# Second feed-forward product before the inner norms: the second tile's own block product is moved from ahead of the last rows to behind the first tile's

## The chip, the core and the metric

The kernel runs on one core of one Trainium2 chip. The metric is the device time of one execution in microseconds (us). Before the change it is 1187.21 us, the median of 3 runs (1186.62 to 1187.24). "Tile" means 128 of the 256 tokens: the first tile is tokens 0 to 127, the second 128 to 255. "Matmul" is one TensorE instruction; in the profile TensorE is PE (its weight loads PEld), VectorE DVE, ScalarE ACT, GpSimd POOL, and SyncE SP.

## The reference, cut to what matters

Two layers of three blocks each. The change concerns the feed-forward block, which is run four times, and the layer norm behind it:

```python
def _swiglu(x, w1, w3, w2):
    return (jax.nn.silu(x @ w1) * (x @ w3)) @ w2

for l in range(DEPTH):                                   # DEPTH = 2
    h = _swiglu(x, ffn_w1[l, 0], ffn_w3[l, 0], ffn_w2[l, 0])
    x = _layernorm(ALPHA * x + 0.5 * h, ln_g[l, 0], ln_b[l, 0])
    h = _mixer(x, ...)                                   # gated token mixers
    x = _layernorm(ALPHA * x + h, ln_g[l, 1], ln_b[l, 1])
    h = _swiglu(x, ffn_w1[l, 1], ffn_w3[l, 1], ffn_w2[l, 1])
    x = _layernorm(ALPHA * x + 0.5 * h, ln_g[l, 2], ln_b[l, 2])
```

x is 256 x 1024, the inner width 2816 (22 blocks of 128). The layer norm is over the 1024 features of a token, so it needs a token's whole row before it can scale any of it.

## The kernel before, in words

**Number format.** Each product is made of three: both operands are split into a high part (float32r) and the rest, and high x high, low x high and high x low are added in PSUM. ACT writes a weight block's high part (`whi`), DVE its low part (`wlo`); both live in two pools of 8 buffers. Weights come by DMA from SP's queue into 4 `raw` buffers.

**The second product of a feed-forward block** is `gemm_seven` (L380). Its output is 2 tiles x 2 halves of 512 columns, collected in four PSUM banks `q[half][tile]`. The first 8 of the 22 inner blocks are done as 2 x 2 blocks with seven products in place of eight (`product`, L372: 12 matmuls of 128x512 each, of which the text calls one a *block product*). One of the sums goes through a side bank `bx`: its value is added on DVE into the token rows `y = xtok` by `ln.fold` (L626), and the last of them, `product(bx, a22, pieces(r1), ...)` with the `fold(1, 0, ...)` behind it, concerns the second tile's first half alone. The other 14 inner blocks are plain rows (`rows`, L405): one call is one weight piece for one tile, 6 matmuls. For the second half of the columns there are 7 such pieces, `rest(1)`; they are all made first (`held`), then the first tile runs over all 7 (42 matmuls), then the second tile (42 matmuls).

**The norm.** `done` calls `Norm.part` (L640): a half of the product is added to `y` on DVE (L647, SCALAR_TENSOR_TENSOR) and its statistics are taken (L651, BN_STATS). With a tile's second half comes `Norm.finish` (L655): BN_AGGR, an inverse square root in small DVE steps (L255 to L261), and the scaled rows (L667). The first tile's first 512 features are turned by four PE transposes (L714), its other half and the second tile's two halves by transposing DMAs (L220, `moved`). Then `affine` (L745) writes the next stage's input `x`: ACT applies gain and bias (L762) and writes the high part (L247), DVE the low part (L249). `self.xlo[0, 0]` is the DVE instruction that writes the low part of the first tile's first 512 features; `part` puts the addition of a second half behind it.

**What comes next.** Behind three of the four feed-forward blocks stands another stage, and its first product (`gemm_b2`, L467, rows by `rows_b` L314, matmuls L283) reads that `x` as the stationary operand: 48 matmuls for the first tile, the first 24 of them over its first 512 features, then 48 for the second tile. The order of instructions on PE is written out by hand; on the other engines it is made by a scheduler that follows priorities, dependences and the `behind` marks. `beat` advances a clock, counted in matmuls, by which the norm's later steps are put between the matmuls.

Of the kernel before, what the change touches and what calls it, by code (L numbers as in the profile page):

```python
# [17 lines left out]
ALU = mybir.AluOpType  # L18
# [5 lines left out]
NT = T // P  # L24
# [30 lines left out]
def trunk(ctx, tc, x, xT, w13a, w13b, w2, wb, wqk, wu, wg, wgr, wbr, wbrr, wo, gateb, gatebr, sgug, sgub, sguwT, sgubias, lam, diffg,  # L55
          lng, lnb, lngT, lnbT, cosT, sinT, out):
    nc = tc.nc
    V, A, G, PE = nc.vector, nc.scalar, nc.gpsimd, nc.tensor
# [15 lines left out]
    def name(s):  # L74
        serial[0] += 1
        return f"{s}_{serial[0]}"

    def bank():
        return psum.tile([P, 512], F32, tag="main", name=name("bank"))

    def side_bank():
        return psum.tile([P, 512], F32, tag="side", name=name("sbank"))
# [41 lines left out]
    def beat(w):  # L124

        clock[0] += w
        for task in list(tasks):
            if task[0] <= clock[0]:
                turn(task)
# [20 lines left out]
    def inline(eng, ins):  # L150
        if line[2]:
            line[eng is V] = ins
        return ins

    def behind(ins):

        return tc.issue_after(ins) if ins is not None else nullcontext()
# [87 lines left out]
    def split(hi, lo, src, eng=V, after=(None, None)):  # L245
        with behind(after[0]):
            a = A.activation(hi, src, AF.Copy).ins  # L247
        with behind(after[1]):
            return a, eng.tensor_tensor(out=lo, in0=src, in1=hi.bitcast(F32), op=ALU.subtract).ins  # L249
# [97 lines left out]
    def halved(v):  # L347
        return v if isinstance(v, list) else [v[:, o : o + HC] for o in range(0, CH, HC)]
# [13 lines left out]
    def pieces(raw):  # L362
        out = []
        for v in halved(raw):
            hi = hi_pool.tile([P, HC], F32R, tag="hi", name=name("whi"))
            lo = lo_pool.tile([P, HC], F32R, tag="lo", name=name("wlo"))
            for eng, ins in zip((A, V), split(hi, lo, v, after=line[:2])):
                inline(eng, ins)
            out.append((hi, lo))
        return out  # L370

    def product(ps, x, w, start, stop):  # L372
        for k in range(4):
            hi, lo = (v[:, k % 2 * 512 : k % 2 * 512 + 512] for v in w[k // 2])
            for n, (y, o) in enumerate(((hi, 0), (lo, 0), (hi, 1))):
                PE.matmul(ps, x[o](k), y, start=start and k == n == 0, stop=stop and k == 3 and n == 2,  # L376
                          skip_group_check=True)
            beat(0.25)

    def gemm_seven(src, xh, xl, sums, ln, done):  # L380

        q = [[bank(), bank()], [side_bank(), bank()]]  # L390
        bx, bz = side_bank(), q[1][0]
        (w11, w21), (w12, w22) = ([s[:, o : o + CH] for o in (0, CH)] for s in src)

        def rest(c):
            for k in range(8, FT, 4):
                nk = min(4, FT - k)
                if c:
                    for j, piece in enumerate(stream(src[c][:, k * 512 : (k + nk) * 512], nk * 512)):
                        yield k + 2 * j, piece
                    continue  # L400
                raw = fetch(src[c][:, k * 512 : (k + nk) * 512], nk * 512)
                for o in range(0, nk * 512, HC):
                    yield k + o // 512, pieces([raw[:, o : o + HC]])[0]

        def rows(t, c, k0, piece, o=0, n=512):  # L405
            for j in range(2):
                k = k0 + j
                hi, lo = (w[:, j * 512 + o : j * 512 + o + n] for w in piece)
                for m, (y, x) in enumerate(((hi, xh), (lo, xh), (hi, xl))):
                    PE.matmul(q[c][t][:, :n] if o == 0 else more[:, :n], x(k, t), y,  # L410
                              start=k == 8 and m == 0 and (c, t) != (1, 0) and not o, stop=k == FT - 1 and m == 2, skip_group_check=True)
            beat(n / 1024)

        def block(t, k0):
            return tuple(lambda k, f=f: f(k0 + k, t) for f in (xh, xl))

        a11, a12, a22 = block(0, 0), block(0, 4), block(1, 4)
        first = rest(0)

        def between():  # L420
            k, piece = next(first)
            for t in range(NT):
                rows(t, 0, k, piece)

        r1 = fetch(w11)
        p1 = pieces(r1)
        r2 = fetch(w12, raw=homes(hi_pool, "hi"))
        product(bx, a11, p1, True, False)
        ln.fold(0, 0, bx, ALU.add, True)
        between()  # L430
        p2 = pieces(fetch(w21))
        plus(r1, r2)
        product(q[0][0], a12, p2, False, False)
        gather(r2, w22)
        r3 = fetch(w22, raw=homes(lo_pool, "lo"))
        between()
        product(bz, sums[0], pieces(r1), True, False)
        ln.fold(1, 1, bz, ALU.add, True)
        between()
        product(bx, sums[1], pieces(plus(r1, r3)), False, False)  # L440
        ln.fold(0, 1, bx, ALU.subtract, True)
        gather(r1, w21)
        between()
        product(bz, sums[3], pieces(r3), False, False)
        between()
        product(bx, sums[2], pieces(r2), False, False)
        ln.fold(1, 1, bx, ALU.subtract, False)
        between()
        between()
        product(bx, a22, pieces(r1), False, True)  # L450
        ln.fold(1, 0, bx, ALU.add, True)
        for t in range(NT):
            done(t, q[0][t], 0, 512)
        held = list(rest(1))
        line[:] = None, None, False
        cuts = ((0, 512),), (((0, 256), (256, 256)) if ln.last else ((0, 512),))
        for t in range(NT):
            for o, n in cuts[t]:
                more = bank() if o else None
                if o:  # L460
                    for m, x in enumerate(ln.kept()):
                        PE.matmul(more[:, :n], ln.unit, x, start=m == 0, stop=False, skip_group_check=True)
                for k, piece in held:
                    rows(t, 1, k, piece, o, n)
                done(t, (more if o else q[1][t])[:, :n], 512 + o, n)

    def gemm_b2(srcs, xh, xl, done, norm=None, second=(0, 1), each=None):  # L467
# [126 lines left out]
    class Norm:  # L594
# [5 lines left out]

        def __init__(self, l, i, scale, eps, after, last=False):
            self.scale, self.eps, self.last, self.done, self.front = scale, eps, last, set(), i
            self.ends, self.xhi, self.xlo, self.rows = [None] * NT, {}, {}, {}
            self.gT, self.bT = (v[:, l, i] for v in (ln_g, ln_b))
            self.y = x_tok
            self.group = 256 if last else 512
            self.st = [sm("st", D // self.group * 6, bufs=2) for _ in range(NT)]
            self.g, self.b = bc_load(lng[l, i], after), bc_load(lnb[l, i], after)
            if last:
                beside(self.halved(), 9)  # L610
                self.minus = s512("minus")
                A.activation(self.minus[:, :P], ident, AF.Copy, scale=-1.0)
                self.eps_t = self.minus[:, 2 * P : 2 * P + 1]
                V.memset(self.eps_t, eps)
                with behind(silu[0]):
                    A.activation(sm("first", 1), mask[:, :1], AF.Sqrt)
            else:
                self.via = []
                self.x = [xs.tile([P, 4, 512], F32R, tag="x", name=name("x")) for _ in range(2)]
# [20 lines left out]
        def part(self, t, c, ps, folded=False):  # L640
            s = slice(c, c + ps.shape[1])
            if self.last and (t, s.stop) == (NT - 1, D):
                V.bn_stats(out=self.st[t][:, c // self.group * 6 : c // self.group * 6 + 6], in_=ps)  # L643
                self.end = ps
                return
            with behind(self.xlo.get((0, 0)) if c else None):
                V.scalar_tensor_tensor(out=self.y[t][:, s], in0=self.y[t][:, s], scalar=1.0 if folded else self.scale,  # L647
                                       in1=ps, op0=ALU.mult, op1=ALU.add)
            for o in range(s.start, s.stop, self.group):
                g = o // self.group * 6  # L650
                V.bn_stats(out=self.st[t][:, g : g + 6], in_=self.y[t][:, o : o + self.group])  # L651
            if self.last and t == NT - 1 and s.stop < D:
                V.tensor_tensor(out=self.y[t][:, s], in0=self.y[t][:, s], in1=self.g[:, s], op=ALU.mult)

# [703 lines left out]
```

## Time and profile before

| | |
|---|---|
| time, median of 3 runs | 1187.21 us (1186.62 to 1187.24) |
| the profiled execution's own time | 1186.85 us |
| its span in the trace | 1185.1 us |
| granted TensorE clock, mean | 1.00 |
| where the three inner `gemm_seven` end and the next stage begins | about 180.4, 591.9 and 766.8 us |
| the last `gemm_seven` (not changed) ends the kernel | from about 1120 us on |

The profile has a page and views of the trace. A line of a timeline gives start, duration, engine, source line, operation, output<-input, and the number of instructions merged into the line; in brackets stands the idle time before it and what ended it. A line of the chain gives start, duration, and what was on the path that ended last; the duration there is net, so that matmuls following each other without a gap show their spacing. Matmul durations in a timeline overlap, since matmuls are pipelined. The time of the execution lies 1.75 us above its span.

### The profile page before, as it was taken

How to read it: one execution, taken by the hardware profiler on the slowest of the kernel's cores; microseconds unless marked ns; L12 is line 12 of the kernel's file. 1: busy time of each engine (PE TensorE's matmuls, PEld its weight loads, DVE VectorE, ACT ScalarE, POOL GpSimd, SP SyncE). 2: the span in 40 equal slices, each digit the busy share in tenths (PEclk: the TensorE clock that was granted, in tenths of full speed). 3: DMA queues.
4: the chain of work that ended last, by engine and by line, in shares of the span. 5: the costliest groups of instructions: out<-in, count | busy, mean ns of one | idle time of the engine just before them, and what ended most of it. 6: DMA issues, size and time to landing. Idle time of an engine off the chain costs nothing.

```text
span 1185.1 us, 16676 instructions
## 1 busy us (share of the span) xinstructions
PE 1180.5 (100%) x5777; PEld 995.0 (84%) x5777; DVE 1013.1 (85%) x1562; ACT 828.1 (70%) x1419; POOL 287.5 (24%) x350
## 2 busy tenths in 40 slices
PE   9999999999999999999999999999999999999998
PEld 8888888888888888888888888888888888888887
DVE  6989989788688989889899889888965989988895
ACT  6688658559955677876667876576788556679761
POOL 1011201247420220051020161003564112102600
PEclk9999999999999999999999999999999999999999
DMA  9869976767865658699668689586666755786881
GB/s 355 265 198 262 287 273 208 266 193 238 246 205 173 227 188 273 187 275 267 239 220 265 190 278 280 198 290 232 212 204 208 250 181 174 247 254 208 273 260 36
DMA packets 129621, 275.10 MB, mean 232 GB/s; under 512 B 89041, under 2 KB 90369, under 8 KB 105473
## 3 DMA queue, kind: packets, MB, share of 16 engines
q1 hardware_dynamic: 121968, 248.67, 63.5%
q0 software_dynamic: 6992, 24.71, 8.7%
q8 instruction: 45, 0.74, 0.2%
q10 hardware_dynamic: 576, 0.66, 0.2%
q14 instruction: 40, 0.32, 0.1%
HBM read 248.05 MB, written 1.05 MB: 210 GB/s over the span
## 4 chain that ended last, share of the span: by engine, by line
PE 99%; DVE 0%; DVEq 0%; issue 0%
PE bank L283 46%; PE bank L295 15%; PE sbank L376 12%; PE bank L410 10%; PE bank L302 8%; PE sbank L410 3%; PE bank L530 2%; PE sbank L1017 1%; PE bank L376 1%; PE sbank L1073 1%; PE sbank L1191 1%; PE sbank L542 0%; PE sbank L1071 0%; PE sbank L714 0%; DVE xtok L701 0%; DVE st L643 0%
## 5 line engine op out<-in xcount | busy, mean ns | idle before, releaser
L197 DVE TENSOR_TENSOR wlo<-raw,whi 128x1024 fp32r<-128x1024 f32 (+1 forms) x346 | 379.4, 1123 | 51.8 <-ACT whi L195 38.0
L195 ACT ACTIVATE whi<-raw 128x1024 fp32r<-128x1024 f32 (+1 forms) x350 | 323.4, 952 | 135.1 <-PE bank L283 43.0
L283 PE MATMUL bank<-whi,x 128*128 128x512 f32 x1224 | 386.4, 390 | 0.0
L283 PEld LDWEIGHTS bank<-whi,x 128*128 128x128 f32 x1224 | 229.8, 188 | 47.8
L283 PE MATMUL bank<-wlo,x 128*128 128x512 f32 x612 | 238.2, 389 | 0.0
L249 DVE TENSOR_TENSOR wlo<-raw,whi 128x1024 fp32r<-128x1024 f32 (+1 forms) x123 | 142.9, 1185 | 20.3 <-ACT whi L247 11.4
L247 ACT ACTIVATE whi<-raw 128x1024 fp32r<-128x1024 f32 (+1 forms) x123 | 121.1, 1003 | 51.2 <-DVE raw L359 23.9
L295 PE MATMUL bank<-x,whi 128*128 128x512 f32 x640 | 153.3, 391 | 0.0
L295 PEld LDWEIGHTS bank<-x,whi 128*128 128x128 f32 x640 | 118.2, 188 | 23.8
L283 PEld LDWEIGHTS bank<-wlo,x 128*128 128x128 f32 x612 | 114.9, 188 | 23.1
L229 POOL COPY seven<-seven 128x512 uint16<-128x512 uint16 x16 | 58.8, 3733 | 135.2 <-ACT whi L195 54.6
L302 PEld LDWEIGHTS bank<-x,wlo 128*128 128x128 f32 x640 | 81.4, 191 | 2.9
L302 PE MATMUL bank<-x,wlo 128*128 128x256 f32 x640 | 82.6, 283 | 0.0
L410 PE MATMUL bank<-whi,hhi 128*128 128x512 f32 (+1 forms) x182 | 68.2, 374 | 0.0
L410 PE MATMUL bank<-whi,hlo 128*128 128x512 f32 (+1 forms) x182 | 67.9, 373 | 0.0
L410 PE MATMUL bank<-wlo,hhi 128*128 128x512 f32 (+1 forms) x182 | 67.9, 373 | 0.0
L993 POOL TENSOR_TENSOR swap<-swap,sin_t 128x512 f32<-128x512 f32 x16 | 26.9, 1680 | 101.2 <-DMA swap<-z 84.4
L757 POOL COPY nvia<-ntwo 128x256 uint16<-128x256 uint16 x20 | 10.0, 547 | 161.2 <-DMA ntwo<-nvia 148.2
L303 ACT ACTIVATE r<-bank 128x256 f32<-128x256 f32 x96 | 34.9, 373 | 16.3 <-PE bank L302 16.1
L376 PE MATMUL sbank<-whi,xhs 128*128 128x512 f32 x128 | 42.0, 389 | 0.0
L410 PEld LDWEIGHTS bank<-whi,hlo 128*128 128x128 f32 x182 | 34.3, 188 | 6.0
L410 PEld LDWEIGHTS bank<-whi,hhi 128*128 128x128 f32 x182 | 34.3, 188 | 6.0
(292 smaller groups left out, 2157.6 us busy)
## 6 DMA issues: line engine op xcount, KB each, us to landing
raw<-in_w13b SPq DMA_DIRECT2D x68, 1024.0 KB, 6.0
raw<-in_w SPq DMA_DIRECT2D x32, 1024.0 KB, 7.0
raw<-in_wb SPq DMA_DIRECT2D x16, 1024.0 KB, 6.7
raw<-in_wqk SPq DMA_DIRECT2D x16, 1024.0 KB, 6.2
home<-in_w13b SPq DMA_DIRECT2D x16, 512.0 KB, 5.9
raw<-in_w13a SPq DMA_DIRECT2D x8, 1024.0 KB, 4.9
home<-in_w SPq DMA_DIRECT2D x16, 512.0 KB, 4.9
raw<-in_wgr SPq DMA_DIRECT2D x8, 1024.0 KB, 5.4
```

What stands on the lines that cost most here:

```text
L195: inline(A, A.activation(h, r, AF.Copy).ins)
L197: low = eng.tensor_tensor(out=w, in0=r, in1=h.bitcast(F32), op=ALU.subtract).ins
L229: eng.tensor_copy(out=o, in_=i)
L247: a = A.activation(hi, src, AF.Copy).ins
L249: return a, eng.tensor_tensor(out=lo, in0=src, in1=hi.bitcast(F32), op=ALU.subtract).ins
L283: PE.matmul(ps, xx, w, start=start and n == 0, stop=stop and n == 2)
L295: PE.matmul(b[-1], hi[:, k * P : (k + 1) * P], xc(k), start=k == 0, stop=False)
L302: PE.matmul(b[n][:, :T], lo[:, k * P : (k + 1) * P], xc(k)[:, :T], start=False, stop=k == KT - 1)
L303: emptied[0] = A.activation(r[:, s], b[n][:, T:], AF.Copy, scale=scale).ins
L376: PE.matmul(ps, x[o](k), y, start=start and k == n == 0, stop=stop and k == 3 and n == 2, skip_group_check=True)
L410: PE.matmul(q[c][t][:, :n] if o == 0 else more[:, :n], x(k, t), y, start=k == 8 and m == 0 and (c, t) != (1, 0) and not o, stop=k == FT - ...
L993: turned_by[0] = G.tensor_tensor(out=s3, in0=s3, in1=s, op=ALU.mult).ins
```

## The change

In the three inner `gemm_seven` (the last one keeps its order), the block product of the second tile and what hangs on it move:

- The first of the 7 pieces of the second half is now run for both tiles at the place where the block product stood (12 matmuls for 12).
- The block product runs between the first tile's last rows and the second tile's. The first tile then has 36 matmuls left in place of 42, and between its end and the end of `gemm_seven` stand 12 + 36 matmuls in place of 42.
- The second tile's `fold` and its first half's `part` (an addition, then BN_STATS) move with it: they are issued behind the third of its six remaining rows, and behind `xlo[0, 0]`.
- The addition of a half is marked to come behind the same tile's last BN_STATS (`counted`), in every norm.

```diff
-        product(bx, a22, pieces(r1), False, True)
-        ln.fold(1, 0, bx, ALU.add, True)
-        for t in range(NT):
+        p4, second = pieces(r1), rest(1)
+
+        if ln.last:
+            product(bx, a22, p4, False, True)
+            ln.fold(1, 0, bx, ALU.add, True)
+        else:
+            k, piece = next(second)
+            for t in range(NT):
+                rows(t, 1, k, piece)
+        for t in range(NT if ln.last else 1):
             done(t, q[0][t], 0, 512)
-        held = list(rest(1))
+        held = list(second)
...
         for t in range(NT):
+            if t and not ln.last:
+                product(bx, a22, p4, False, True)
             for o, n in cuts[t]:
...
-                for k, piece in held:
+                for j, (k, piece) in enumerate(held):
                     rows(t, 1, k, piece, o, n)
+                    if t and j == 2 and not ln.last:
+                        with behind(ln.xlo[0, 0]):
+                            ln.fold(1, 0, bx, ALU.add, True)
+                        done(1, q[0][1], 0, 512)
...
-            with behind(self.xlo.get((0, 0)) if c else None):
+            with behind(self.xlo.get((0, 0)) if c else None), behind(self.counted.get(t)):
                 V.scalar_tensor_tensor(out=self.y[t][:, s], in0=self.y[t][:, s], scalar=1.0 if folded else self.scale,
                                        in1=ps, op0=ALU.mult, op1=ALU.add)
...
-                V.bn_stats(out=self.st[t][:, g : g + 6], in_=self.y[t][:, o : o + self.group])
+                self.counted[t] = V.bn_stats(out=self.st[t][:, g : g + 6], in_=self.y[t][:, o : o + self.group]).ins
```

How the instructions now stand is shown for the first of the three places; the other two read alike but for the buffers' numbers. Lines of the changed kernel are 13 higher from L460 on (L647 is L660 there, L651 L664, L629 L642, L762 L775).

PE, where the first tile's last rows end. Bank 1216 collects the first tile's second half, bank 1217 the second tile's, side bank 1218 is `bx`. Before:

```order
L410 MATMUL sbank_1216<-whi_1548,hhi_153 128x512
L410 MATMUL sbank_1216<-wlo_1549,hhi_153 128x512
L410 MATMUL sbank_1216<-whi_1548,hlo_164 128x512
L410 MATMUL bank_1217<-whi_1518,hhi_150 128x512
L410 MATMUL bank_1217<-wlo_1519,hhi_150 128x512
L410 MATMUL bank_1217<-whi_1518,hlo_161 128x512
```

And now:

```order
L410 MATMUL sbank_1216<-wlo_1546,hhi_153 128x512
L410 MATMUL sbank_1216<-whi_1545,hlo_164 128x512
L376 MATMUL sbank_1218<-whi_1491,hhi_148 128x512
L376 MATMUL sbank_1218<-wlo_1492,hhi_148 128x512
L376 MATMUL sbank_1218<-whi_1491,hlo_159 128x512
```

The twelve matmuls of the block product (L376) stand here now, three of them shown, and the second tile's rows begin behind them; the four transposes of the first tile then stand 18 matmuls ahead of the end of `gemm_seven`, where before 12 came after them.

DVE, around the write of the low part of the first tile's first 512 features (`x_1212`); `xtok_144` is the second tile's `y`, `st_1205` its statistics. Before:

```order
L197 TENSOR_TENSOR wlo_1788<-raw_1779,whi_1787 128x512 x2
L249 TENSOR_TENSOR x_1212<-xf_1654,x_1212 128x4x128
L647 SCALAR_TENSOR_TENSOR xtok_144<-xtok_144,bank_1217 128x512
L651 BN_STATS st_1205<-xtok_144 128x6
L658 BN_AGGR mv_1675<-st_1205 128x2
```

And now:

```order
L197 TENSOR_TENSOR wlo_1788<-raw_1779,whi_1787 128x512 x2
L249 TENSOR_TENSOR x_1212<-xf_1645,x_1212 128x4x128
L642 SCALAR_TENSOR_TENSOR xtok_144<-xtok_144,sbank_1218 128x512
L660 SCALAR_TENSOR_TENSOR xtok_144<-xtok_144,bank_1215 128x512
L664 BN_STATS st_1205<-xtok_144 128x6
L660 SCALAR_TENSOR_TENSOR xtok_144<-xtok_144,bank_1217 128x512
L664 BN_STATS st_1205<-xtok_144 128x6
L671 BN_AGGR mv_1675<-st_1205 128x2
```

The fold, the first half's addition and its BN_STATS stand between the first tile's write and the second half's addition; before they stood some twenty rows higher, among the weight splits.

ACT, around the same features (`xf_...` is the PE transposes' result with gain and bias). Before:

```order
L195 ACTIVATE whi_1817<-raw_1809 128x512 x2
L762 ACTIVATE xf_1654<-sbank_1649,ln_b,ln_g 128x128 x4
L247 ACTIVATE x_1212<-xf_1654 128x4x128
L759 ACTIVATE nvia_1616<-ntwo_1757 128x256 x2
L762 ACTIVATE nvia_1616<-nvia_1616,ln_b,ln_g 128x128 x3
```

And now:

```order
L775 ACTIVATE xf_1645<-sbank_1640,ln_b,ln_g 128x128 x4
L195 ACTIVATE whi_1817<-raw_1809 128x512
L247 ACTIVATE x_1212<-xf_1645 128x4x128
L772 ACTIVATE nvia_1607<-ntwo_1757 128x256 x2
L775 ACTIVATE nvia_1607<-nvia_1607,ln_b,ln_g 128x128 x3
```

One half of a weight split of the next stage (`whi_1817`) has moved between the gain-and-bias step and the high part's write.

More of the change, by code (lines that the diff above doesn't have):

```diff
@@ L602, in __init__ @@
             self.scale, self.eps, self.last, self.done, self.front = scale, eps, last, set(), i
-            self.ends, self.xhi, self.xlo, self.rows = [None] * NT, {}, {}, {}
+            self.ends, self.xhi, self.xlo, self.rows, self.counted = [None] * NT, {}, {}, {}, {}
             self.gT, self.bT = (v[:, l, i] for v in (ln_g, ln_b))
```

## Prediction

> **What bounds the kernel now.** I read the page first (busy shares, clock, chain), then who waited on PE, then the chain in order of time, then DVE's and ACT's timelines around the three places where a changed `gemm_seven` ends.
>
> ```profile
> span 1185.1 us, 16676 instructions
> PE 1180.5 (100%) x5777; PEld 995.0 (84%) x5777; DVE 1013.1 (85%) x1562; ACT 828.1 (70%) x1419; POOL 287.5 (24%) x350
> PEclk9999999999999999999999999999999999999999
> PE 99%; DVE 0%; DVEq 0%; issue 0%
> PE sbank L542 <- DVE warm L538: 1.0, 1, 1.0
> ```
>
> The chain that ended last is PE alone, at full clock, and the longest PE wait listed is 1.0 us at the very start. A faster kernel would need fewer matmuls or closer ones; the change has neither (4352 PE rows before and after). What it can do is add or remove short waits. For those I look at net durations in the chain:
>
> ```profile
> 27.47 10.88 PE bank L283 x48
> 158.26 2.72 PE sbank L376 x12
> 160.99 9.52 PE sbank L410 x42
> 177.31 0.43 PE sbank L714 x4
> 177.74 2.77 PE bank L410 x12
> 180.52 21.93 PE bank L283 x96
> 592.03 27.36 PE bank L283 x120
> 767.00 21.83 PE bank L283 x96
> ```
>
> 48 matmuls take 10.88 us, 0.2267 us each; so do the other stretches. The next stage's first matmuls are the exception: 96 should take 21.76 us and take 21.93 and 21.83, 120 should take 27.20 and take 27.36. So PE loses 0.17, 0.16 and 0.07 us at the three places, 0.40 in all, waiting for the first tile's `x`. **That 0.40 us (0.03%) is all the change can win.**
>
> The Trainium skill (Perfetto Trace Analysis, section Identifying the Most-Contended Engine) says that the busy share of matmuls is no good measure of how near TensorE is to its limit, and that the share of weight loads is better. By that, 84% here would leave room in which PE could catch up after a wait, and the sum below would go towards nothing. By the rows it can't: no stretch of these matmuls runs closer than 0.2267 us. I go by the rows.
>
> **The change part by part.**
>
> *PE work: nothing.* Twelve matmuls change places with twelve (first weight piece for both tiles against the block product).
>
> *The first tile's norm: early enough now.* Between its last row and the end stand 48 matmuls in place of 42, and its transposes stand 18 from the end in place of 12. That is 6 x 0.2267 = 1.36 us earlier. The wait of 0.17, 0.16 and 0.07 us at the stage's start was for DVE's low part:
>
> ```profile
> 175.98 1.15 ACT L195 ACTIVATE whi<-raw 128x512 fp32r<-128x512 f32 x2 [0.21 <-PE bank L410]
> 179.32 0.63 ACT L247 ACTIVATE x<-xf 128x512 fp32r<-128x512 f32 x1
> 179.99 0.80 DVE L249 TENSOR_TENSOR x<-xf,x 128x512 fp32r<-128x512 f32 x1 [0.41 <-ACT x L247]
> 180.36 0.39 PE L283 MATMUL bank<-lhi,x 128*128 128x512 f32 x1
> 180.71 0.67 DVE L647 SCALAR_TENSOR_TENSOR xtok<-xtok,bank 128x512 f32<-128x512 f32 x1
> ```
>
> It ends at 180.79; the stage's third matmul is the first that reads it, would otherwise start at 180.36 + 2 x 0.2267 = 180.81, and lost 0.17. So a matmul goes on some 0.17 us behind the data that its weight load needs; I use that as the price of the hand-over below. Against the 1.36 us gained, ACT now does one half of a weight split ahead of `x`'s high part (half of the row at 175.98, about 0.55). Net the low part is 0.8 us earlier, and this wait goes.
>
> *The second tile's norm: later.* This is the term that decides. DVE works its queue in order. Before, the second half's addition (180.71) followed the first tile's low part directly. Now three instructions stand between. The rows of the same operations, where they stood before:
>
> ```profile
> 158.43 0.68 DVE L647 SCALAR_TENSOR_TENSOR xtok<-xtok,bank 128x512 f32<-128x512 f32 x1
> 159.15 0.69 DVE L651 BATCH_NORM_STATS2 st<-xtok 128x6 f32<-128x512 f32 x1
> 164.42 0.69 DVE L651 BATCH_NORM_STATS2 st<-xtok 128x6 f32<-128x512 f32 x1
> 165.02 2.48 DVE L197 TENSOR_TENSOR llo<-raw,lhi 128x512 fp32r<-128x512 f32 x4
> ```
>
> An instruction that needs the one ahead starts 0.72 us behind it (158.43 to 159.15), one that doesn't 0.60 (164.42 to 165.02). So, in the time of before: low part from 179.99 - 1.36 + 0.55 = 179.18; fold 0.72 later (as 180.71 followed 179.99), 179.90; the first half's addition at 180.62; BN_STATS at 181.34; the second half's addition at 181.94 instead of 180.71. **The second tile's norm starts 1.23 us late.** The 2 us of work that were hidden among the weight splits, while DVE had time, are now in the one place where DVE's order decides.
>
> *How much of it is hidden.* The second tile's chain runs on DVE to the end: statistics, inverse root, scaling, four weight splits queued ahead, then the halves that come back from the transposing DMAs.
>
> ```profile
> 186.29 2.49 DVE L197 TENSOR_TENSOR wlo<-raw,whi 128x512 fp32r<-128x512 f32 x4
> 188.70 0.48 DVE L574 TENSOR_TENSOR lampr<-lam 128x128 f32<-128x128 f32 x2
> 189.10 0.91 DVE L755 COPY nvia<-ntwo 128x256 uint16<-128x256 uint16 x4
> 772.66 2.49 DVE L197 TENSOR_TENSOR wlo<-raw,whi 128x512 fp32r<-128x512 f32 x4
> 775.24 0.92 DVE L755 COPY nvia<-ntwo 128x256 uint16<-128x256 uint16 x4
> ```
>
> At the first place two instructions of the setup (L574, 0.40 us from start to the copies' start) now stand behind the copies, so the delay there is 0.83. At the third the copies started 0.09 us after the splits ended (775.15 to 775.24), where at the first place the next instruction starts 0.08 before their end; 0.17 of idle time takes up that much, and 1.06 is left. At the second it is the whole 1.23.
>
> What meets PE is the second tile's third and fourth block of features, which ACT writes last ahead of PE's need:
>
> ```profile
> 191.99 0.39 ACT L247 ACTIVATE x<-nvia 128x256 fp32r<-128x256 f32 x1
> 603.10 0.39 ACT L247 ACTIVATE x<-nvia 128x256 fp32r<-128x256 f32 x1
> 778.14 0.39 ACT L247 ACTIVATE x<-nvia 128x256 fp32r<-128x256 f32 x1
> 191.40 0.39 PE L283 MATMUL bank<-lhi,x 128*128 128x512 f32 x1
> 602.91 0.39 PE L283 MATMUL bank<-lhi,x 128*128 128x512 f32 x1
> 777.79 0.39 PE L283 MATMUL bank<-lhi,x 128*128 128x512 f32 x1
> 195.46 0.43 DVE L249 TENSOR_TENSOR x<-nvia,x 128x256 fp32r<-128x256 f32 x1
> ```
>
> The three PE rows are the second tile's first matmul at each place; the seventh is the first that reads these blocks, 1.36 us later: 192.76, 604.27, 779.15. ACT ends at 192.38, 603.49, 778.53. The slack is 0.38, 0.78 and 0.62 us. It already holds the wait of before, so the gain above is in it. Per place: delay + hand-over - slack.
>
> - first: 0.83 + 0.17 - 0.38 = 0.62
> - second: 1.23 + 0.17 - 0.78 = 0.62
> - third: 1.06 + 0.17 - 0.62 = 0.61
>
> Together **+1.85 us**. The second tile's last two blocks are ready at 195.89 (last row above) and first read 30 matmuls in, at 198.20: 2.3 us ahead, and 1.2 less is still enough.
>
> *The weight pieces: hidden.* The first piece is now needed at 158.3 instead of 161.0.
>
> ```profile
> 151.24 2.35 DVE L197 TENSOR_TENSOR wlo<-raw,whi 128x1024 fp32r<-128x1024 f32 x2
> 159.66 1.06 ACT L195 ACTIVATE whi<-raw 128x1024 fp32r<-128x1024 f32 x1 [0.30 <-PE sbank L376]
> 160.63 1.13 ACT L195 ACTIVATE lhi<-raw 128x512 fp32r<-128x512 f32 x2
> 176.04 12.29 SPq L220 DMA_TRANSPOSE ntwo<-nvia  x3
> 188.37 7.45 SPq L173 DMA_DIRECT2D raw<-in_wqk  x4
> ```
>
> DVE has split it by about 152.5; the cover is over 5 us. The block product's two pieces are held longer, and the seventh piece, which used to take a buffer that the block product freed (159.66), now takes the first piece's, free at 161.0, and stands behind two of the next stage's splits (1.13 us) on ACT: 161.0 + 1.1 + 1.1 + 1.2 for DVE is 164.4, needed after five rows, at 161.0 + 6.8 = 167.8. Cost nothing, 3.4 us of cover. SP's order does not change, but its transposes come 1.2 us later and the four weight fetches behind them too; these weights are for matmuls behind the 96 that end at 180.52 + 21.93 = 202.45 us, so I take nothing; without that cover it would be 1.2 at each place, 3.6 us.
>
> *The mark on additions behind BN_STATS* leaves the order of the other norms on DVE as it was: nothing.
>
> **Sum.** 1186.85 (the profiled execution's own time) + 1.85 = 1188.7 us. The median of the runs shown is 0.36 above that execution; from there it would be 1189.1.
>
> **The rivals.**
>
> 1. *The additions fit in after all* (not slower). If the fold starts 1.23 us earlier than I have it, the delay is zero and only the gain is left: 1186.85 - 0.40 = 1186.5 us. The point from which it decides is a start of the fold at 178.7. For it: DVE idles 0.41 us ahead of the low part (row 179.99), and ACT's moved half may fall into ACT's own idle time. Against: the order has the fold behind the low part, and that can't come before the transposes.
> 2. *The delay is larger.* If the transposing DMAs meet other transfers, or the 3.6 us of fetches is not covered, it is 1.85 + up to 3.6 more: 1190 to 1192.3. For it: the fetches begin right behind the transposes (rows 176.04 and 188.37), so a later start moves both towards the next stage's need. Against: between 176 and 188 us the SP queue issues transposes only.
> 3. *The clock.* The Trainium skill (TensorE: Matmul & The Clock Gate, section A second HAM failure mode: psum-queue depth-cycling) tells of short PE pauses that make the clock gate fall to half speed and back. That would be a mechanism of its own here: if each of the three pauses cost a stretch as long as this kernel's warm-up matmuls, some 4 us at half speed, it would add 2 us a place. The time would be about 1194.7. Against: pauses of 0.17 us at these places, and 1.0 at the start, left the granted clock at full in all forty slices.
>
> ```profile
> 1.05 4.13 PE sbank L542 x37
> ```
>
> **How the numbers follow.** About 0.2% (2.4 us) is what a measurement of this kernel tells from no change; above 1187.21 that is 1189.6. Forecast 0.71, rival 1 0.14, rival 2 0.11, rival 3 0.02, something else faster 0.02. The forecast's own spread: each place may be 0.3 off in either term, 1187.6 to 1189.9, and about a seventh of it (0.10) is above 1189.6. So slower 0.10 + 0.11 + 0.02 = 0.23, same 0.61 + 0.14 = 0.75, faster 0.02. The range takes in rival 1 and the lower part of rival 2: 1186.5 to 1190.4.
>
> **What the profile would show.** Right: the chain's first stretch of L283 after each changed `gemm_seven` with no excess in its first 48 matmuls and 0.6 to 0.8 at the 49th to 57th; DVE with the second half's addition about 1.2 us behind the end of `gemm_seven` further than before; PE waits on ACT or DVE for `x`. Wrong: no PE excess at those places (rival 1), PE waiting for `whi` or `wlo` in the rows of L410 (a weight piece late), granted clock under 1.00 (rival 3), or a time under 1184.8, which no row here explains.

## The result, and the profile after

The changed kernel takes 1188.44 us (median of 21 runs, 1188.16 to 1189.19), the kernel before 1186.63 us beside it (21 runs, 1186.32 to 1187.24). The ratio is 1.0015, with a 95% interval of 1.0009 to 1.0021: 1.8 us slower. The profiled execution took 1188.43 us, 1.58 more than that of before.

The first view is the page of the changed kernel:

```profile
span 1186.6 us, 16672 instructions
PE 1181.5 (100%) x5777; PEld 994.2 (84%) x5777; DVE 1013.7 (85%) x1562; ACT 828.1 (70%) x1419; POOL 294.1 (25%) x350
PEclk9999999999999999999999999999999999999999
PE 97%; DVE 2%; ACT 1%; issue 0%; DVEq 0%; ACTq 0%
```

Busy shares and clock are as before and tell nothing. The last line does: 3% of the chain, 99% PE before, now runs over DVE and ACT. Who waited is seen on PEld, since `x` is the stationary operand and the weight load is what waits. The rows give what was waited for, then us in total, times, and the longest. First after, then before:

```profile
PEld bank L283 <- ACT x L247: 2.5, 6, 0.5
PEld bank L283 <- DVE x L249: 1.1, 6, 0.2
```

```profile
PEld bank L283 <- DVE x L249: 0.8, 3, 0.3
```

Three waits became twelve, and ACT's high part is the larger releaser now. Such a wait counts from when the weight load could have run, and weight loads run ahead of PE; so 3.6 us here are not 3.6 us lost. What PE lost is read from its own timeline, here around the first place:

```profile
180.07 0.39 PE L283 MATMUL bank<-lhi,x 128*128 128x512 f32 x1
...
180.53 0.62 PE L283 MATMUL bank<-lhi,x 128*128 128x512 f32 x2
...
190.73 0.39 PE L283 MATMUL bank<-whi,x 128*128 128x512 f32 x1
191.17 0.50 PE L283 MATMUL bank<-lhi,x 128*128 128x512 f32 x1
...
192.47 0.81 PE L283 MATMUL bank<-lhi,x 128*128 128x512 f32 x2
193.12 0.40 PE L283 MATMUL bank<-llo,x 128*128 128x512 f32 x1
...
195.43 0.39 PE L283 MATMUL bank<-lhi,x 128*128 128x512 f32 x1
```

The stage starts at 180.07, the third matmul follows on time at 180.53, and the 48th starts at 190.73, 47 x 0.2267 = 10.66 later: nothing is lost in the first tile. The 49th, the second tile's first, starts 0.44 behind it in place of 0.23. The row at 192.47 holds two matmuls. The second is the 55th; it starts at 192.47 + 0.81 - 0.50 = 192.78 (a matmul that waited is given 0.50 us, as at 191.17), 0.08 late, and the 56th (193.12) another 0.11 late. The last row is the 66th matmul, which is 15.36 behind the start. At full pace it is 65 x 0.2267 = 14.73, so the stage has lost 0.63 us. Read in the same way it is 0.61 and 0.60 at the other two places, 1.84 in all (as the prediction said it would show: nothing in the first 48, 0.6 to 0.8 from the 49th on); before it was 0.17, 0.16 and 0.07, all at the third and fourth matmul. **The net, 1.44 us, is what the three places explain of the 1.58 between the profiled executions.** DVE and ACT show where it comes from; the two ACT rows come last:

```profile
178.80 0.69 DVE L249 TENSOR_TENSOR x<-xf,x 128x512 fp32r<-128x512 f32 x1 [0.86 <-ACT x L247]
179.41 0.68 DVE L642 SCALAR_TENSOR_TENSOR xtok<-xtok,sbank 128x512 f32<-128x512 f32 x1
180.12 0.69 DVE L660 SCALAR_TENSOR_TENSOR xtok<-xtok,bank 128x512 f32<-128x512 f32 x1
180.85 0.69 DVE L664 BATCH_NORM_STATS2 st<-xtok 128x6 f32<-128x512 f32 x1
181.46 0.67 DVE L660 SCALAR_TENSOR_TENSOR xtok<-xtok,bank 128x512 f32<-128x512 f32 x1
182.89 0.21 DVE L671 BATCH_NORM_AGGREGATE mv<-st 128x2 f32<-128x12 f32 x1
```

```profile
177.61 0.64 ACT L195 ACTIVATE whi<-raw 128x512 fp32r<-128x512 f32 x1
192.34 0.39 ACT L247 ACTIVATE x<-nvia 128x256 fp32r<-128x256 f32 x1
```

Fold, addition and BN_STATS stand between the low part and the second half's addition, which starts 1.39 us behind the stage's start (181.46 less 180.07), 0.35 before (180.71 less 180.36). The second tile's third and fourth block of features are written on ACT by 192.73. The 55th matmul, the first that reads them, starts 0.05 behind that, and the 56th loses another 0.11: 0.16 us for the hand-over.

Below, "lost" is always the time that the three stages behind a changed `gemm_seven` take beyond 0.2267 us a matmul: 0.40 us before, 1.84 after. The second number to follow is when BN_AGGR starts, since the second tile's norm hangs on it: 2.82 us behind the stage's start (182.89 less 180.07), before 1.79 (182.15 less 180.36):

```profile
182.15 0.21 DVE L658 BATCH_NORM_AGGREGATE mv<-st 128x2 f32<-128x12 f32 x1
```

### The profile page after: what moved, and what is told of

Same layout as the page of the kernel before. It is cut to its first block, busy times and chain, and to the rows that moved or that the text cites. A ratio compares the mean times of both kernels' runs of the same rounds, so it can differ in the third digit from the quotient of the medians.

```text
span 1186.6 us, 16672 instructions
## 1 busy us (share of the span) xinstructions
PE 1181.5 (100%) x5777; PEld 994.2 (84%) x5777; DVE 1013.7 (85%) x1562; ACT 828.1 (70%) x1419; POOL 294.1 (25%) x350
## 4 chain that ended last, share of the span: by engine, by line
PE 97%; DVE 2%; ACT 1%; issue 0%; DVEq 0%; ACTq 0%
PE bank L283 44%; PE bank L295 15%; PE sbank L376 12%; PE bank L410 9%; PE bank L302 8%; PE sbank L410 3%; PE bank L543 2%; PE sbank L1030 1%; PE bank L376 1%; PE sbank L1086 1%; PE sbank L1204 1%; DVE wlo L197 0%; PE sbank L555 0%; PE sbank L1084 0%; ACT xf L775 0%
## 5 line engine op out<-in xcount | busy, mean ns | idle before, releaser
L229 POOL COPY seven<-seven 128x512 uint16<-128x512 uint16 x16 | 64.4, 4092 | 127.3 <-ACT whi L195 53.4
L376 PE MATMUL sbank<-whi,xhs 128*128 128x512 f32 x128 | 42.0, 389 | 0.0
L283 PE MATMUL bank<-lhi,x 128*128 128x512 f32 x120 | 39.7, 396 | 0.2
```

Source lines behind the costliest of these rows:

```text
L229: eng.tensor_copy(out=o, in_=i)
L283: PE.matmul(ps, xx, w, start=start and n == 0, stop=stop and n == 2)
```

## The experiments

**Theory:** the order of instructions on DVE between the first tile's low part and the second half's addition makes the second tile late. **Rivals:** the new order on PE costs it (with the weight pieces held longer and the later transposes); or another chain ends last at that wait. Each kernel has its edit against the changed kernel unless it says otherwise, and ran beside the kernel before: 1186.57 us (21 runs) for fold_early, act_half_behind, twice_stats and old_pe_late_add, 1186.68 us (33 runs) for the other four.

### fold_early: the fold alone in DVE's idle time

```diff
-                        with behind(ln.xlo[0, 0]):
+                        with behind(ln.ends[0]):
                             ln.fold(1, 0, bx, ALU.add, True)
-                        done(1, q[0][1], 0, 512)
+                        with behind(ln.xlo[0, 0]):
+                            done(1, q[0][1], 0, 512)
```

> The changed kernel with the fold alone put ahead: it stands behind the first tile's plane copies on DVE, before the six weight splits and x's low part, in time in which DVE idles 0.86 us; the first half's addition and BN_STATS stay behind the low part. Theory (DVE's queue between the low part and the second half's addition makes the second tile late): the second half's addition comes 0.6 us earlier, the excess of 0.56, 0.55 and 0.55 us in L283 at the second tile's blocks goes, the time falls by 1.5 to 1.7 us to 1186.7-1186.9. Rival (the matmul order, the longer held weight pieces or the later transposes are the cause): unchanged, 1188.4.

Measured: 1186.99 us (11 runs), ratio to before 1.0001 (0.9993 to 1.0010). DVE first, then the three stages in the chain (96, 120 and 96 matmuls, 21.76, 27.20 and 21.76 us at full pace):

```profile
178.65 0.94 DVE L249 TENSOR_TENSOR x<-xf,x 128x512 fp32r<-128x512 f32 x1 [0.27 <-ACT x L247]
179.51 0.67 DVE L661 SCALAR_TENSOR_TENSOR xtok<-xtok,bank 128x512 f32<-128x512 f32 x1
182.27 0.21 DVE L672 BATCH_NORM_AGGREGATE mv<-st 128x2 f32<-128x12 f32 x1
```

```profile
180.08 21.87 PE bank L283 x96
591.54 27.32 PE bank L283 x120
766.47 21.87 PE bank L283 x96
```

The idle time ahead of the low part fell from 0.86 to 0.27 us, the fold is gone from behind it, and lost are 0.11, 0.12 and 0.11 us. I had expected the loss to go whole, and the time lies just above the range. BN_AGGR came 0.47 us earlier, not 0.6, because the low part takes 0.94 us here in place of 0.69. The order on PE, the held pieces and the transposes are the changed kernel's own, so they are not what costs 1.8 us.

### act_half_behind: ACT's half split behind x

```diff
-                with behind(first[0]), behind(line[0]):
+                with behind(first[0]), behind(line[0]), behind(wait if o + p == width - sub else None):
...
+                wait=norm.xhi[0, 0] if norm and norm.front != 1 and n == 3 else None
```

> The changed kernel with ACT's half weight split (0.52 us, ahead of x's high part) put behind the high part. Theory: high part, low part and everything behind them on DVE come 0.52 us earlier, the excess at the second tile's blocks falls from 0.55 to 0.05 us a place, the time by 1.4 to 1.6 us to 1186.8-1187.0; if a later half split makes the third or fourth weight chunk late, a wait of up to 0.5 us a place shows at L283 instead. Rival (ACT's order is off the path): unchanged, 1188.4.

Measured: 1186.89 us (11 runs), ratio 1.0002 (0.9993 to 1.0010). The three stages in the chain:

```profile
179.99 22.00 PE bank L283 x96
591.58 27.47 PE bank L283 x120
766.66 22.05 PE bank L283 x96
```

Lost are 0.24, 0.27 and 0.29 us. So a half of a weight split on ACT, 0.52 us ahead of the high part, was worth 1.04 us over the three places. The time fell into the expected range, but the places kept 0.24 to 0.29 us where 0.05 was expected. The high part starts 1.52 us behind the start of the gain-and-bias step (176.00 to 177.52), in the changed kernel 1.89 (176.24 to 178.13): it is 0.37 us earlier, not 0.52. No weight chunk was late.

### both_early: both edits

The two edits above together.

> The changed kernel with both edits of fold_early and act_half_behind: the fold ahead of the weight splits, and ACT's half split behind x's high part. Theory: the second half's addition comes 0.8 to 1.1 us earlier than in the changed kernel, all waits at the second tile's blocks go, and the first tile's wait of before (0.15, 0.14, 0.03 us) stays gone: 0.3 us under before, 1186.2 to 1186.5. Rival (fold_early and act_half_behind, 1187.0 and 1186.9 with waits no longer than those of before, point to a cost of 0.3 to 0.4 us that lies outside these three places): 1186.8 to 1187.1.

Measured: 1186.95 us (11 runs), ratio 1.0001 (0.9992 to 1.0010). The chain, with a stretch of 24 matmuls in the attention stage:

```profile
180.29 21.76 PE bank L283 x96
275.48 5.63 PE bank L283 x24
592.18 27.20 PE bank L283 x120
766.99 21.76 PE bank L283 x96
```

All three stages run at full pace, and nothing is lost there: the 0.40 us that the prediction gave as the most to be won is won. The time does not show it. Its rival's number came out (1186.8 to 1187.1), though the interval takes in both. Part of the reason is in the trace: PE waited at the first attention's value product, 80 us later, which neither kernel shows there, and the 24 matmuls at 275.48 took 0.16 longer than before (5.47).

```profile
PEld sbank L1086 <- issue: 0.5, 1, 0.5
```

### fold_in_norm: without the order behind the low part

```diff
-                        with behind(ln.xlo[0, 0]):
-                            ln.fold(1, 0, bx, ALU.add, True)
+                        ln.fold(1, 0, bx, ALU.add, True)
```

> The changed kernel without the order of the fold behind x's low part: fold, first half's addition and BN_STATS then stand among the small steps of the first tile's inverse root on DVE. Theory: nothing is left between the low part and the second half's addition, so the wait at the 49th to 57th matmul goes; but the first tile's norm is 1.4 to 2.1 us longer, its low part and its blocks from the transposing DMA come that much later than in the changed kernel, and a wait of 0.2 to 1.0 us a place appears in the first 24 matmuls of L283 instead: 1187.2 to 1189.8. Rival (DVE has room there, the small steps leave gaps that take the three instructions): 1186.4 to 1186.9, no wait over 0.15 us in these stages.

Measured: 1186.87 us (11 runs), ratio 1.0000 (0.9991 to 1.0008). The scheduler puts the three instructions among the first tile's small steps, the fold (first row) between two of them; the scaling and the low part follow. Below it the chain:

```profile
171.85 0.68 DVE L641 SCALAR_TENSOR_TENSOR xtok<-xtok,sbank 128x512 f32<-128x512 f32 x1
...
174.19 1.00 DVE L679 TENSOR_SCALAR xtok<-xtok,mv,nwy 128x512 f32<-128x512 f32 x2
...
179.39 0.69 DVE L249 TENSOR_TENSOR x<-xf,x 128x512 fp32r<-128x512 f32 x1
```

```profile
180.37 21.76 PE bank L283 x96
592.62 27.20 PE bank L283 x120
767.43 21.76 PE bank L283 x96
```

My expectation missed, and the rival's was right: nothing is lost at any place. From the first tile's last addition to the scaling it takes 5.16 us (169.03 to 174.19) in place of 3.75 (168.90 to 172.65), so the first tile's norm is 1.41 us longer. But most of that goes into the 0.86 us of idle time ahead of the low part, which stands only 0.45 later, 0.82 us ahead of the stage's start. **What costs the time is the order behind `xlo[0, 0]`, not the moved product.**

### no_mark: without `counted`

```diff
-            with behind(self.xlo.get((0, 0)) if c else None), behind(self.counted.get(t)):
+            with behind(self.xlo.get((0, 0)) if c else None):
```

> The changed kernel without the mark of additions behind BN_STATS: on DVE the second half's addition stands directly behind the first half's, and both BN_STATS behind it. Theory: what counts is when the second tile's statistics are done, and the same six instructions stand ahead of that, so nothing changes: 1188.2 to 1188.7, an excess of 0.5 to 0.6 us a place. Rival (the wait is set by the start of the second half's addition, which comes 0.6 us earlier): 1186.8.

Measured: 1187.42 us (11 runs), ratio 1.0005 (0.9996 to 1.0014). DVE, then the chain:

```profile
180.13 0.68 DVE L642 SCALAR_TENSOR_TENSOR xtok<-xtok,sbank 128x512 f32<-128x512 f32 x1
180.84 1.28 DVE L660 SCALAR_TENSOR_TENSOR xtok<-xtok,bank 128x512 f32<-128x512 f32 x2
182.05 1.28 DVE L664 BATCH_NORM_STATS2 st<-xtok 128x6 f32<-128x512 f32 x2
183.36 0.21 DVE L671 BATCH_NORM_AGGREGATE mv<-st 128x2 f32<-128x12 f32 x1
```

```profile
5.18 22.73 PE bank L543 x96
180.95 22.10 PE bank L283 x96
593.81 27.55 PE bank L283 x120
768.97 22.10 PE bank L283 x96
```

Neither held. Lost are 0.34, 0.35 and 0.34 us, 1.03 in place of 1.84. The same instructions stand ahead of BN_AGGR, but they take 3.23 us from the fold's start (180.13 to 183.36) in place of 3.48 (179.41 to 182.89). With the mark an addition is followed by the BN_STATS that needs it, 0.70 to 0.73 us behind; without it the two additions and the two BN_STATS follow each other in pairs that don't need one another, 0.60 us apart. The profiled execution took 1189.08, 1.66 above the median: its first 96 matmuls took 22.73, and it has the wait at the value product too (1.1 us).

### twice_stats: one instruction more

```diff
                         done(1, q[0][1], 0, 512)
+                        with behind(ln.counted[1]):
+                            ln.counted[1] = V.bn_stats(out=ln.st[1][:, 0:6], in_=ln.y[1][:, :512]).ins
```

> The changed kernel with the second tile's first BN_STATS done twice, so a fourth instruction of 0.60 to 0.72 us stands on DVE between the low part and the second half's addition. Theory: each of the three waits at the second tile's blocks grows by the whole instruction, from 0.55 to 1.2 us, 1.8 to 2.2 us in all, 1190.2 to 1190.6. Rival (another chain, the transposing DMAs or ACT, ends last at that wait): less than 0.2 us per place, 1188.4 to 1189.0.

Measured: 1190.75 us (5 runs), ratio 1.0033 (1.0021 to 1.0046). DVE, and PE's first second-tile matmul:

```profile
181.81 0.70 DVE L479 BATCH_NORM_STATS2 st<-xtok 128x6 f32<-128x512 f32 x1
182.42 0.67 DVE L662 SCALAR_TENSOR_TENSOR xtok<-xtok,bank 128x512 f32<-128x512 f32 x1
```

```profile
192.13 0.50 PE L283 MATMUL bank<-lhi,x 128*128 128x512 f32 x1 [0.61 <-ACT x L247]
```

The instruction set BN_AGGR back from 2.82 to 3.55 us, and the loss rose from 0.63 to 1.31 at the first place and from 1.84 to 3.92 in all: 0.73 us of delay, 0.69 a place, as expected; the median lies 0.15 above the expected range. No other chain takes up the wait.

### old_pe_late_add: the old order on PE, the new one on DVE

Against the kernel before; the block product stays where it was, and only what DVE does with it moves:

```diff
-        ln.fold(1, 0, bx, ALU.add, True)
-        for t in range(NT):
+        if ln.last:
+            ln.fold(1, 0, bx, ALU.add, True)
+        for t in range(NT if ln.last else 1):
             done(t, q[0][t], 0, 512)
...
-                for k, piece in held:
+                for j, (k, piece) in enumerate(held):
                     rows(t, 1, k, piece, o, n)
+                    if t and j == 4 and not ln.last:
+                        with behind(ln.xlo[0, 0]):
+                            ln.fold(1, 0, bx, ALU.add, True)
+                        done(1, q[0][1], 0, 512)
```

(`counted` is in it as well.)

> The order of matmuls, transposes and weight pieces of before; only the fold and the first half's addition of the second tile are held back behind the first tile's low part, as in the changed kernel. Theory: DVE has the same three instructions in the same place and no 1.36 us head start, so the second half's addition is 2.0 us late instead of 1.0 to 1.2; per place 2.04 less 0.40 (first) or 0 or 0.17 (third), plus 0.17, less the slack of 0.38, 0.78, 0.62: 1.4 us, 4.3 us in all, 1190.5 to 1190.9. Rival (the order on PE and what hangs on it costs the time): as before, 1186.6.

Measured: 1191.90 us (5 runs), ratio 1.0042 (1.0028 to 1.0056). DVE:

```profile
182.43 0.67 DVE L652 SCALAR_TENSOR_TENSOR xtok<-xtok,bank 128x512 f32<-128x512 f32 x1
183.87 0.21 DVE L663 BATCH_NORM_AGGREGATE mv<-st 128x2 f32<-128x12 f32 x1
```

The addition starts 2.39 us behind the stage (180.04). Lost are 1.61, 1.61 and 1.49 us, 4.31 more than before, where 4.3 was expected; the profiled execution was 4.40 above that of before, the median 5.3, which is 1.0 above the expected range and not explained by the three places. So the new order on PE is a help: with its 1.36 us of head start the same order on DVE costs 1.44 us in place of 4.31.

### second_place_only: the change at one place

```diff
-        p4, second = pieces(r1), rest(1)
+        p4, second, stays = pieces(r1), rest(1), ln.last or ln.front != 2
...
-        if ln.last:
+        if stays:
```

(and `stays` for `ln.last` at the other places of the function.)

> The change made at the second place alone (the second feed-forward of the first layer), the others as before. Theory (each place pays by itself): the second place shows an excess of 0.55 us at the second tile's blocks and none at its start, the first and the third the waits of before (0.15, 0.03); 0.4 us over before, 1186.9 to 1187.2. Rival (a fixed cost of the program, or one that the places hand on): the full 1188.4, or none.

Measured: 1187.10 us (11 runs), ratio 1.0003 (0.9994 to 1.0011). The chain keeps the rows of before at the first and third place:

```profile
180.13 21.93 PE bank L283 x96
602.58 16.89 PE bank L283 x72
767.08 21.84 PE bank L283 x96
```

At the second the chain breaks off and comes back to PE with the second tile's first matmul; 0.62 us are lost there, 0.17 and 0.08 at the others. Each place pays by itself.

### One line through all of them

BN_AGGR's start behind the stage's start and the loss, both at the first place, then the loss of the three places together:

| kernel | BN_AGGR | lost, first place | lost, all three | profiled execution, less 1186.85 | median, less that of before |
|---|---|---|---|---|---|
| fold_in_norm | 1.65 | 0.00 | 0.00 | +0.36 | +0.19 |
| before | 1.79 | 0.17, first tile | 0.40 | 0 | 0 |
| second_place_only | 1.80 | 0.17, first tile | 0.87 | 0.00 | +0.42 |
| both_early | 1.96 | 0.00 | 0.00 | -0.17 | +0.27 |
| fold_early | 2.35 | 0.11 | 0.34 | -0.40 | +0.42 |
| act_half_behind | 2.47 | 0.24 | 0.80 | -0.14 | +0.32 |
| no_mark | 2.57 | 0.34 | 1.03 | +2.23 | +0.74 |
| changed | 2.82 | 0.63 | 1.84 | +1.58 | +1.81 |
| twice_stats | 3.55 | 1.31 | 3.92 | +3.90 | +4.18 |
| old_pe_late_add | 3.83 | 1.61 | 4.71 | +4.40 | +5.33 |

The loss is BN_AGGR's start less 2.22 us, within 0.03 in every row from 2.35 on, whatever moved it: a fold, a split on ACT, a mark, a repeated instruction or PE. (In second_place_only the changed place is the second: BN_AGGR 2.81, lost 0.62.) Up to 2.22 the second tile costs nothing; before it stood at 1.79, and its 0.40 us were the first tile's.

## Why the prediction was right, point by point

- *Most to be won 0.40 us, PE cannot catch up.* Right: both_early and fold_in_norm win exactly that at the three places in the trace, and no more. (The trace has 5777 matmuls in either kernel; the 4352 rows that the prediction counts stand in no view of it.) No stretch of them made up for a wait. The Trainium skill (Perfetto Trace Analysis, section Identifying the Most-Contended Engine) recommends the share of weight loads, beside a count of the arithmetic done, for judging how near TensorE is to its limit. Read as room to catch up, the 84% of both kernels misleads here.
- *First tile's norm early enough.* Right: its wait went at all three places. The low part starts 1.27 us ahead of the stage in place of 0.37, 0.90 earlier where 0.81 was worked out.
- *DVE's order decides.* Right in mechanism, and mis-sized: the second half's addition is 1.04 us later against the stage's start, not 1.23. 0.09 is the low part; 0.11 is that the fold does not need the low part and starts 0.61 behind it, where I took 0.72.
- *What of it is hidden.* The two instructions at the first place took up 0.40: BN_AGGR is 1.03 later there, the copies (189.10 before, 189.44 now) 0.63. Net, 0.46, 0.45 and 0.53 us were lost where 0.62, 0.62 and 0.61 were forecast. The total of 1.85 met the medians' 1.81, and that closeness is luck: the three places hold 1.44 of it, 0.41 less than forecast, and 0.37 lies elsewhere and was not forecast. The hand-over (0.17 taken, 0.16 measured) was right. The chances went by 2.4 us as what can be told from no change; 21 runs of each kernel tell 1.8 us.
- *The third and fourth block.* Half the story: the 49th matmul waits first, for the first two blocks, and the 55th again. Only the last one counts for the sum, since what is lost at the 49th moves the 55th as well.
- *The `counted` mark costs nothing.* The prediction says so of the other norms, and there DVE's order is indeed as before. In the three changed places the mark is not free: with the order behind `xlo[0, 0]` in place, 0.81 of the 1.84 us are its doing (no_mark). The sum had this in, without a name, since it was worked out from the order with the mark; what the prediction did not see is that the mark makes each BN_STATS follow directly on the addition that it needs.
- *Weight pieces and fetches hidden.* Right in the changed kernel. With more delay they are not: in twice_stats and old_pe_late_add the 38th and 39th matmul lose 0.14 to 0.27 us a place, for a low part of the next stage's weights (`wlo`) whose split on DVE stands behind the scaling of the second tile.
- *Rival 1* needed the fold earlier, and the order was the argument against it; with that order taken away it happened in the trace (fold_in_norm), while the median stayed 0.19 above the kernel before. *Rival 2* did not: the transposes moved with the norm, and PE lost no more than BN_AGGR's line gives. *Rival 3*, the clock, did not happen: the granted clock is 1.00 in every run, with pauses of up to 0.8 us at each place in twice_stats and old_pe_late_add. The oscillation of which the Trainium skill tells (TensorE: Matmul & The Clock Gate, section A second HAM failure mode: psum-queue depth-cycling) did not show here.

**What stays open.** The medians differ from that of before by -0.1 to 1.0 us more than the loss does. Three things in the profiled executions are as large and lie elsewhere: the program's first 96 matmuls (22.01 us in the changed kernel, 22.30 before, 22.73 in no_mark), the time from the chain's last instruction to the span's end (3.1 us in the changed kernel, 2.7 before), and the wait at the attention's value product. For the changed kernel the first two nearly cancel: 1.44 less 0.29, plus 0.39, is 1.54 of the 1.58 us between the profiled executions. What makes them differ was not tried. The wait at the value product was in three of the eight experiments:

```profile
PEld sbank L1083 <- issue: 0.9, 1, 0.9
```

This is fold_in_norm's. Against the kernel before, the scheduler changed a few places on DVE in that stage in every version but second_place_only; whether that causes it was not tried. No version's median lies below that of the kernel before.

## What to carry to other kernels

Where a chain of small steps on one engine feeds the next stage, find one point on it (here BN_AGGR) and how late it may be; an edit costs nothing up to there and its whole delay beyond. An order written down to protect one chain is paid by what stands behind it: try the edit without it, and put movable work into idle time that the trace names (0.86 us ahead of the low part). And count not only the instructions ahead of that point but which of them need the one before.

## What the runs showed that I had not expected

- On DVE a 128x512 addition and its BN_STATS start 0.70 to 0.73 us apart, two that don't need each other 0.60 to 0.61 us. Reordering the same instructions brought BN_AGGR 0.25 us forward a place.
- Three such instructions (0.68 us each, 2.04 us busy) put among the small steps of the inverse root lengthened that chain by 1.41 us: the small steps leave gaps on DVE. The fold starts 0.19 us behind the step ahead of it (171.66 to 171.85), where a step of the same kind is followed by the next small step 0.31 behind (171.10 to 171.41).
- In the changed kernel a late stationary operand is listed as a wait of PEld, not of PE; only the longer pauses of twice_stats and old_pe_late_add are listed on PE too (0.6 us each). PE starts some 0.05 us behind the write and loses another 0.11 at the next matmul.
